# Layer 1 attention with every value product in plain single precision, keys in the index queries' buffer, and the sample's digit counts summed by a block transpose

## The chip, the cores and the metric

The kernel runs on one core of a Trainium2 chip. The metric is the device time of one execution in microseconds (us), the median of three runs. Instructions are issued on five engines: TensorE (PE; its weight loads are shown apart as PEld), VectorE (DVE), ScalarE (ACT), GpSimd (POOL) and SyncE (SP, which only issues DMAs).

## The reference, cut to what matters

One step of a two-layer decoder on a prompt of 1024 tokens and 8 sample tokens with 1024 cached tokens each. Layer 1 is the one that changes: 16 query heads over 4 key/value heads of width 64, where each query sees only the 256 keys that an indexer scores highest.

```python
score = jnp.einsum('bqhk,bqh->bqk', jax.nn.relu(dots), wi.astype(jnp.float32))
causal = kpos[None, None, :] <= qpos[None, :, None]
_, idx = lax.top_k(jnp.where(causal, score, -jnp.inf), topk)
...
s = jnp.einsum('bqngd,bqknd->bqngk', qg, k_sel).astype(jnp.float32) * (HEAD_DIM ** -0.5)
...
o = jnp.einsum('bqngk,bqknd->bqngd', p, v_sel)
```

The prompt has 8 blocks of 128 queries; a block i sees i+1 blocks of keys. Everything is in single precision.

## The kernel before

All work of layer 1 runs in streams: Python generators that yield an estimated time after each piece. A driver always continues the stream with the least virtual time, and a scheduler that simulates the program then fixes the order of instructions on each engine and the buffer of each tile. A tile waits for a free buffer of its kind. Each engine then runs its list strictly in that order.

The streams that meet around the change:

- The input projection (gen_main, dense_cols) multiplies in three products of split operands (L339 to L341, tiles d, xh, xl, whif, wlof). The weights of the next column tile are split ahead by ACT (whif) and DVE (wlof). The last tiles are queries, then keys (post_k), then values (post_v). The rotation of queries and keys runs on POOL (tiles raw, shf).
- The indexer (gen_idx, idx_scores) scores query blocks 2 to 7. top_select then finds each row's 256th score by 31 bisection steps, in pairs of blocks (2 and 3, 4 and 5, 6 and 7); each step is a count (L1983 on DVE, or an ACT pass with sign, tile tjk) and some operations on 128x2 elements (L226, L229, tile small). The result is a mask per block, written over the scores (tile sc).
- The sample stream (gen_dsa_dec) does the same for the 8 sample tokens, in 8 digit steps of 4 bits: 16 partitions of each sample try the 16 values of a digit, a count over 1025 scores (L2253) tells which hold, and a product with a constant matrix on PE (L2258, tile grpc) sums the outcomes of the 16 partitions. After the digits come ranks (transposed on PE at L2292, the rows "b<-small,hk"), one-hot lists and their product (L2314), then gathers of the chosen rows and their attention. The work area is the tile hk.
- The attention of the prompt (gen_attn, dsa_units, Unit) runs 32 units, query block i by key/value head g, in order of i. steps_a makes the scores (L530) and adds the mask (L533). steps_b transposes the exponentials in groups of one key block and four heads (L251, tile t), copies them out of PSUM (tile ph), and pv multiplies them with the values. The steps of a unit are interleaved with those of the unit before it.

Two forms of pv stand in the kernel. For blocks 0 to 4 (PLAIN) it is one single-precision product per group, 64 value columns by 512 (L2089, two records in the trace), and fin divides by the row sums, which are broadcast by a DMA through DRAM (d_ls, rv). For blocks 5 to 7 it is folded: ph holds a rounded high part and the low rest (made by ACT and by DVE, or by ACT and POOL through the tile pf where SPARE says so), the values stand in VS as high and low parts side by side, two reduced-precision products per group give 128 rows (L2093), and merge_out adds the halves, with the row sums brought over by two PE transposes (tiles rx, r). Blocks 5 to 7 have 4 x (6+7+8) = 84 groups in 12 units, blocks 0 to 4 have 60 groups in 20 units.

Four-part buffers (H, six of them): four hold the normalized activations, one the index queries and index keys (HX[0], tile hx, free once the last score is made, flag hx_free), one the sample's work area (HX[1], tile hk, free after L2314, flag hk_free). KS (split keys) and VS (split values) each need one later. The code for the keys is written after hk_free, that for the values after hx_free and the keys.

The out-projection (out1, on PE as L339 to L341 again) begins when all units and the samples are done (flags l1.att and l1.dec).

Of the kernel before, what the change touches and what calls it, by code (L numbers as in the profile page):

```python
# [32 lines left out]
def _consts():  # L33
# [32 lines left out]
    c["grp16"] = ((p[:, None] // 16 == p[None, :] // 16) & (p[:, None] % 16 >= 1)).astype(f)  # L66
# [9 lines left out]
def _r(ap):  # L76
    return ap.bitcast(F32)
# [17 lines left out]
SPARE = {3: (1,), 4: (1,), 5: (1, 3), 6: (1, 3), 7: (1, 3)}  # L95
BFC = True
PLAIN = range(5)
PMUL = ()
RXP = True
# [60 lines left out]
def build(tc, I, O, C):  # L160
    nc = tc.nc
    with ExitStack() as ctx:
# [1624 lines left out]
        def post_k(t, raw):  # L1787
            yield from rope(raw)
            nc.gpsimd.tensor_copy(out=K1[:, t], in_=raw[:, S:T])
            yield from need("hk_free")  # L1790
            if t == 0:
                KS[0] = H(F32R, "ks1")
            for e in range(2):
                split_stack(KS[0][:, 2 * t + e], raw, e, 0, S, gt)
            yield 2500.0
            flags.add("l1.k%d" % t)
            yield from nat_out(raw, O["dsa_kv_p"][0, 0, :, 0], t, O["dsa_kv_s"][0, :, 0, 0])

        def post_v(t, raw):
            yield 500.0  # L1800
            yield from need("l1.k1", "hx_free")
            if t == 0:
                VS[0] = H(F32R, "vs1")
            g = nat_out(raw, O["dsa_kv_p"][0, 0, :, 1], t, O["dsa_kv_s"][0, :, 0, 1],
                        [VS[0][:, 2 * t + e, :S].rearrange("p (i f) -> p i f", i=8) for e in range(2)], flip=False,
                        vn=VN1[:, t * 128:(t + 1) * 128], keep=VF)
            yield next(g)
            yield next(g)
            yield next(g)
            flags.add("l1.v%d" % t)  # L1810
            yield from g
# [228 lines left out]
        def dsa_units():  # L2040
# [8 lines left out]
            def make(i, g):  # L2049
# [21 lines left out]

                fold = i not in PLAIN
                d["u"] = 4 * i + g

                def pv(gr, ph):
                    kb = gr["kb"]
                    if kb == 0:
                        pst["o", i, g] = bank("o")
                        nc.vector.reciprocal(out=d["ls"], in_=d["ls"])
                        if fold:  # L2080
                            rx = pst["rx", i, g] = V([128, 4, 64], F32, "rx")
                            (nc.gpsimd if RXP else nc.vector).tensor_copy(out=rx, in_=d["ls"].unsqueeze(2).to_broadcast([128, 4, 64]))
                        else:
                            rv = pst["rx", i, g] = V([128, 512], F32, "rv")
                            dma(out=d_ls[i, g], in_=d["ls"])
                            dma(out=rv[:64], in_=d_ls[i, g].rearrange("q h -> (q h)").partition_broadcast(64))
                    po = pst["o", i, g]
                    if not fold:
                        mm(po[:64], lhsT=VF[g // 2][:, kb, 64 * (g % 2):64 * (g % 2) + 64], rhs=ph, start=(kb == 0), stop=(kb == i))  # L2089
                        return 860.0  # L2090
                    vs = VS[0][:, g, kb * 128:(kb + 1) * 128]
                    for x in range(2):
                        mm(po, lhsT=vs, rhs=ph[:, x], start=(kb + x == 0), stop=(kb == i and x == 1))  # L2093
                    return 430.0

                def fin():
# [4 lines left out]
                    if fold:  # L2101
                        yield from merge_out(ov[:, 0], ov[:, 1], lambda a: rx[:, 2 * a:2 * a + 2].rearrange("p e d -> p (e d)"),
                                             dh, dl, None)
                    else:
                        rw = rx[:64].rearrange("p (q a e) -> p e a q", a=2, e=2)
                        tm = V([128, 2, 128], F32, "tm")
                        pool = d["u"] % 8 in PMUL
                        if pool:
                            oc = V([128, 512], F32, "oc")
                            act(oc[:64], o[:64])  # L2110
                            ov = oc.rearrange("p (a e q) -> p e a q", a=2, e=2)
                            yield 500.0
                        for e in range(2):
                            (gt if pool else tt)(tm[64 * e:64 * e + 64], ov[:64, e], rw[:, e], MUL)
                        yield 700.0
                        act(dh, tm)
                        gt(dl, tm, _r(dh), SUB)
# [3 lines left out]
                u = Unit([tile_(hh) for hh in range(4)], groups, pv, start, fin, SPARE.get(i, ()) if fold else None)  # L2121
# [17 lines left out]
        def gen_dsa_dec():  # L2139
# [93 lines left out]
            grp = V([128, 128], F32, "grpc")  # L2233
            dma(out=grp, in_=C["grp16"])
# [11 lines left out]
            for step in range(8):  # L2246
# [8 lines left out]
                ts(cn, cn, TOPK - 0.5, None, ALU.is_ge)  # L2255
                yield DY
                p = bank()
                late(mm(p[:, 0:1], lhsT=grp, rhs=cn, start=True, stop=True))  # L2258
                yield 700.0
                sh_ = 28 - 4 * step  # L2260
                if step == 0:
                    ts(sf, p[:, 0:1], 7.5, -16.0, ALU.is_ge, MUL)
                    tt(sf, sf, p[:, 0:1], ADD)
                    ts(sh, sf, float(1 << sh_), None, MUL)
                else:
                    ts(sh, p[:, 0:1], float(1 << sh_), None, MUL)
# [20 lines left out]
            yield 26000  # L2287
# [23 lines left out]
            yield 4000  # L2311
# [310 lines left out]
```

## Time and profile before

| what | value |
|---|---|
| median of 3 runs | 2840.72 us (2839.03 to 2842.0) |
| the profiled execution, by the clock of the runs | 2849.54 us |
| its span, first to last instruction | 2847.5 us |
| busy share of PE, DVE, ACT, POOL | 90%, 79%, 47%, 47% |
| mean granted TensorE clock | 0.953 of full speed |

The profiled execution is 8.8 us above the median. A row of a view names line, engine and operation, then output <- inputs by tile names and the shape. "Idle before" is the time an engine stood still just before an instruction, put down to what ended it. All times in rows are in us from the start of the span, single durations in ns where a row says mean or min/median/max.

### The profile page before, as it was taken

The page shows a single profiled execution, that of the slowest core. Times are in us where ns is not written, and L with a number is a line of the kernel's source. Part 1 is how long each engine was busy: PE and PEld are TensorE (multiplying, and loading weights), DVE is VectorE, ACT ScalarE, POOL GpSimd, SP SyncE. Part 2 cuts the span into 40 slices and gives each one's busy share as a digit, 9 for nine tenths or more (in the row PEclk, how much of TensorE's full clock was granted, in tenths as well). Part 3 has the DMA queues.
Part 4 walks back from the last instruction along what each step waited for, and adds up shares of the span by engine and source line. Part 5 has one row for each costly group of instructions (what it writes and reads, how often), then busy time and mean ns, then how long its engine had stood idle before and what let it go on. Part 6 is the DMA issues. An engine that isn't in the chain of part 4 may idle for free.

```text
span 2847.5 us, 48497 instructions
## 1 busy us (share of the span) xinstructions
PE 2560.3 (90%) x17916; PEld 2391.2 (84%) x17916; DVE 2245.4 (79%) x4125; ACT 1330.8 (47%) x2726; POOL 1339.5 (47%) x992
## 2 busy tenths in 40 slices
PE   7988888989999899999888757999978999899998
PEld 6977788989999898999887743557978999898998
DVE  4476887778777889996469997998468887899995
ACT  4235756444433533332356566779434344533331
POOL 2375454245565557630445434224144656567630
PEclk8989999999999999999989878999989999999999
DMA  4844567303444633333353324311312343643431
GB/s 131 267 148 141 163 212 236 129 30 115 151 138 145 205 122 130 130 111 101 83 167 103 121 74 114 90 58 38 112 38 101 139 148 138 213 134 125 136 105 60
DMA packets 272095, 363.30 MB, mean 128 GB/s; under 512 B 25184, under 2 KB 200456, under 8 KB 271604
## 3 DMA queue, kind: packets, MB, share of 16 engines
q1 hardware_dynamic: 217124, 290.48, 32.0%
q0 software_dynamic: 15120, 49.81, 5.3%
q10 hardware_dynamic: 39616, 19.93, 2.4%
q8 instruction: 141, 2.31, 0.3%
q14 instruction: 94, 0.77, 0.1%
HBM read 252.19 MB, written 108.00 MB: 126 GB/s over the span
## 4 chain that ended last, share of the span: by engine, by line
PE 49%; DVE 20%; issue 5%; ACT 3%; DMA 2%; POOL 2%; SPq 0%; DVEq 0%; POOLq 0%; another core or an unknown queue 0%; ACTq 0%
PE d L1491 11%; PE d L1492 10%; PE d L1493 10%; DVE fdu L218 4%; PE d L341 3%; PE d L339 3%; PE d L340 3%; PE s L530 2%; PE t L251 2%; PE o L2089 1%; DVE xT L218 1%; DVE tjk L1983 1%; DVE x1a L218 1%; PE o L2093 1%; DVE fd L218 1%
## 5 line engine op out<-in xcount | busy, mean ns | idle before, releaser
L221 POOL TENSOR_TENSOR fraw<-fraw,small 128x1024 f32<-128x1024 f32 x64 | 137.9, 2160 | 196.7 <-DMA fraw<-in_ffn_w 163.0
L218 DVE TENSOR_TENSOR xT<-xT,d 128x258 f32<-128x258 f32 (+1 forms) x472 | 185.9, 424 | 52.9 <-PE d L341 32.8
L1491 PE MATMUL d<-xoph,fs 128*128 128x258 f32 x768 | 219.3, 286 | 8.6 <-ACT z L215 7.5
L1492 PE MATMUL d<-xoph,fs 128*128 128x258 f32 x768 | 218.3, 284 | 2.3 <-DVE xoph L218 2.3
L1493 PE MATMUL d<-xoph,fs 128*128 128x258 f32 x768 | 218.0, 284 | 2.1 <-DVE fs L218 2.1
L339 PE MATMUL d<-xh,whif 128*128 128x344 f32 (+1 forms) x616 | 201.7, 328 | 1.7 <-ACT xh L215 0.9
L341 PE MATMUL d<-xh,wlof 128*128 128x344 f32 (+1 forms) x616 | 197.2, 325 | 4.6 <-DVE wlof L218 4.6
L340 PE MATMUL d<-xl,whif 128*128 128x344 f32 (+1 forms) x616 | 200.3, 325 | 0.0
L221 POOL TENSOR_TENSOR z<-z 128x516 f32<-128x516 f32 x112 | 170.5, 1522 | 32.2 <-DMA d_zp<-z 21.9
L339 PE MATMUL d<-xh,whi 128*128 128x344 f32 x504 | 171.6, 341 | 10.9 <-ACT whi L215 5.6
L215 ACT ACTIVATE s<-s,small 128x128 f32<-128x128 f32 (+7 forms) x192 | 149.4, 782 | 65.9 <-DVE small L533 61.4
L341 PE MATMUL d<-xh,wlo 128*128 128x344 f32 x504 | 166.6, 333 | 12.0 <-DVE wlo L218 11.9
L340 PE MATMUL d<-xl,whi 128*128 128x344 f32 x504 | 168.6, 335 | 0.0
L218 DVE TENSOR_TENSOR fdu<-fraw,fdu 128x256 fp32r<-128x256 f32 x168 | 161.3, 971 | 0.0
L1491 PE MATMUL d<-xop,fl 128*128 128x258 f32 x512 | 147.2, 288 | 14.6 <-ACT fl L215 14.6
L1491 PEld LDWEIGHTS d<-xoph,fs 128*128 128x128 f32 x768 | 145.9, 190 | 10.3 <-ACT z L215 9.0
L1491 PE MATMUL d<-zoph,fdu 128*128 128x258 f32 x448 | 129.4, 291 | 23.8 <-DVE xT L218 12.1
L251 PE MATMUL t<-small,s 128*128 128x128 f32 x864 | 139.6, 280 | 12.1 <-DVE small L533 7.3
L1493 PEld LDWEIGHTS d<-xoph,fs 128*128 128x128 f32 x768 | 146.4, 191 | 2.7 <-DVE fs L218 2.5
L1492 PEld LDWEIGHTS d<-xoph,fs 128*128 128x128 f32 x768 | 146.1, 190 | 3.0 <-DVE xoph L218 3.0
L1493 PE MATMUL d<-xop,fl 128*128 128x258 f32 x512 | 145.9, 286 | 2.9 <-DVE fl L218 2.9
L1492 PE MATMUL d<-xop,fl 128*128 128x258 f32 x512 | 146.6, 286 | 0.0
(484 smaller groups left out, 9913.1 us busy)
## 6 DMA issues: line engine op xcount, KB each, us to landing
fraw<-in_ffn_w SPq DMA_DIRECT2D x120, 512.0 KB
zr<-d_zp SPq DMA_DIRECT2D x98, 516.0 KB
d_zp<-z POOLq DMA_DIRECT2D x56, 516.0 KB
kp<-in_cache_fox_kv SPq DMA_DIRECT2D x64, 256.0 KB
vp<-in_cache_fox_kv SPq DMA_DIRECT2D x64, 256.0 KB
q1b<-d_q ACTq DMA_DIRECT2D x32, 512.0 KB
d_zp<-z SPq DMA_DIRECT2D x28, 516.0 KB
wraw<-in_ab_w_in SPq DMA_DIRECT2D x21, 512.0 KB
```

Source lines behind the costliest of these rows:

```text
L215: return nc.scalar.activation(out=out, in_=in_, func=func, **kw)
L218: return nc.vector.tensor_tensor(out=out, in0=a, in1=b, op=op)
L221: return nc.gpsimd.tensor_tensor(out=out, in0=a, in1=b, op=op)
L251: return nc.tensor.transpose(out, in_, ident[:n, :n])
L339: mm(ps, lhsT=wh, rhs=ah, start=(j == 0), stop=False)
L340: mm(ps, lhsT=wh, rhs=al, start=False, stop=False)
L341: i = mm(ps, lhsT=wl, rhs=ah, start=False, stop=(j == last))
L530: mm(p[:, :m], lhsT=lh[x], rhs=ks[:, k0:k0 + m], start=(x == 0), stop=(x == 1 and not dg))
L1491: mm(o, lhsT=wh[:, k], rhs=hi[:, cols], start=(start and k == 0), stop=False, skip_group_check=not start)
L1492: mm(o, lhsT=wh[:, k], rhs=lo[:, cols], start=False, stop=False, skip_group_check=not start)
L1493: i = mm(o, lhsT=wl[:, k], rhs=hi[:, cols], start=False, stop=(k == nk - 1), skip_group_check=not start)
L1983: nc.vector.tensor_scalar(out=jk[:, 1, :n], in0=sj, scalar1=th, scalar2=None, op0=op, op1=ADD, accum_out=cnt[:, j:j + 1])
```

## The change

All blocks take the plain form of pv: the folded form, VS, SPARE and merge_out's use in layer 1 go. The keys' code is written after hx_free in place of hk_free. In the digit steps the PE product over 16 partitions goes; DVE spreads the outcome over 32 columns, transposes 32x32 blocks, multiplies by a constant and sums. Two estimates in the sample stream, after the ranks and after the one-hot lists, are longer by 6000 ns each, which places what follows later among the other streams.

```diff
--- before.py
+++ after.py
@@ -63,7 +63,8 @@
     c["bm8x64"] = np.ascontiguousarray(c["bm64"].T)
     c["bm64x128"] = (bh[:, None] // 8 == p[None, :] // 16).astype(f)
     c["bm8x128"] = (b8[:, None] == p[None, :] // 16).astype(f)
-    c["grp16"] = ((p[:, None] // 16 == p[None, :] // 16) & (p[:, None] % 16 >= 1)).astype(f)
+    f32 = np.arange(32)
+    c["grp32"] = ((p[:, None] % 32 // 16 == f32[None, :] // 16) & (f32[None, :] % 16 >= 1)).astype(f)
     c["bd16"] = (p[:, None] // 16 == p[None, :] // 16).astype(f)
     c["iot"] = np.concatenate([np.broadcast_to(np.arange(16, dtype=f), (128, 16)), p[:, None].astype(f)], 1)
     dig = np.zeros((128, 8), np.int64)
@@ -92,11 +93,7 @@
 ZSUB, ZLA = ("dpdpdpd", "p" * 7), 3
 UPE, DNE = ("dddd", "ddddddd"), ("pppp", "ddddddd")
 DNU = "vaavbbv"
-SPARE = {3: (1,), 4: (1,), 5: (1, 3), 6: (1, 3), 7: (1, 3)}
 BFC = True
-PLAIN = range(5)
-PMUL = ()
-RXP = True
 COP = "aad"
 NF = "p"
 KTE = "aa"
@@ -1787,7 +1784,7 @@
         def post_k(t, raw):
             yield from rope(raw)
             nc.gpsimd.tensor_copy(out=K1[:, t], in_=raw[:, S:T])
-            yield from need("hk_free")
+            yield from need("hx_free")
             if t == 0:
                 KS[0] = H(F32R, "ks1")
             for e in range(2):
@@ -1798,11 +1795,7 @@
 
         def post_v(t, raw):
             yield 500.0
-            yield from need("l1.k1", "hx_free")
-            if t == 0:
-                VS[0] = H(F32R, "vs1")
             g = nat_out(raw, O["dsa_kv_p"][0, 0, :, 1], t, O["dsa_kv_s"][0, :, 0, 1],
-                        [VS[0][:, 2 * t + e, :S].rearrange("p (i f) -> p i f", i=8) for e in range(2)], flip=False,
                         vn=VN1[:, t * 128:(t + 1) * 128], keep=VF)
             yield next(g)
             yield next(g)
@@ -2069,56 +2062,35 @@
                 groups = [dict(tr=[(hh * 128, lambda hh=hh, kb=kb: sm[hh][:, kb * 128:(kb + 1) * 128]) for hh in range(4)],
                                w=512, kb=kb) for kb in range(i + 1)]
 
-                fold = i not in PLAIN
-                d["u"] = 4 * i + g
 
                 def pv(gr, ph):
                     kb = gr["kb"]
                     if kb == 0:
                         pst["o", i, g] = bank("o")
                         nc.vector.reciprocal(out=d["ls"], in_=d["ls"])
-                        if fold:
-                            rx = pst["rx", i, g] = V([128, 4, 64], F32, "rx")
-                            (nc.gpsimd if RXP else nc.vector).tensor_copy(out=rx, in_=d["ls"].unsqueeze(2).to_broadcast([128, 4, 64]))
-                        else:
-                            rv = pst["rx", i, g] = V([128, 512], F32, "rv")
-                            dma(out=d_ls[i, g], in_=d["ls"])
-                            dma(out=rv[:64], in_=d_ls[i, g].rearrange("q h -> (q h)").partition_broadcast(64))
+                        rv = pst["rx", i, g] = V([128, 512], F32, "rv")
+                        dma(out=d_ls[i, g], in_=d["ls"])
+                        dma(out=rv[:64], in_=d_ls[i, g].rearrange("q h -> (q h)").partition_broadcast(64))
                     po = pst["o", i, g]
-                    if not fold:
-                        mm(po[:64], lhsT=VF[g // 2][:, kb, 64 * (g % 2):64 * (g % 2) + 64], rhs=ph, start=(kb == 0), stop=(kb == i))
-                        return 860.0
-                    vs = VS[0][:, g, kb * 128:(kb + 1) * 128]
-                    for x in range(2):
-                        mm(po, lhsT=vs, rhs=ph[:, x], start=(kb + x == 0), stop=(kb == i and x == 1))
-                    return 430.0
+                    mm(po[:64], lhsT=VF[g // 2][:, kb, 64 * (g % 2):64 * (g % 2) + 64], rhs=ph, start=(kb == 0), stop=(kb == i))
+                    return 860.0
 
                 def fin():
                     o, rx = pst.pop(("o", i, g)), pst.pop(("rx", i, g))
                     ov = o.rearrange("p (a e q) -> p e a q", a=2, e=2)
                     qs, hx, t0 = slice(i * 128, (i + 1) * 128), g // 2, 2 * g % 4
                     dh, dl = XH[hx][:, t0:t0 + 2, qs], XL[hx][:, t0:t0 + 2, qs]
-                    if fold:
-                        yield from merge_out(ov[:, 0], ov[:, 1], lambda a: rx[:, 2 * a:2 * a + 2].rearrange("p e d -> p (e d)"),
-                                             dh, dl, None)
-                    else:
-                        rw = rx[:64].rearrange("p (q a e) -> p e a q", a=2, e=2)
-                        tm = V([128, 2, 128], F32, "tm")
-                        pool = d["u"] % 8 in PMUL
-                        if pool:
-                            oc = V([128, 512], F32, "oc")
-                            act(oc[:64], o[:64])
-                            ov = oc.rearrange("p (a e q) -> p e a q", a=2, e=2)
-                            yield 500.0
-                        for e in range(2):
-                            (gt if pool else tt)(tm[64 * e:64 * e + 64], ov[:64, e], rw[:, e], MUL)
-                        yield 700.0
-                        act(dh, tm)
-                        gt(dl, tm, _r(dh), SUB)
+                    rw = rx[:64].rearrange("p (q a e) -> p e a q", a=2, e=2)
+                    tm = V([128, 2, 128], F32, "tm")
+                    for e in range(2):
+                        tt(tm[64 * e:64 * e + 64], ov[:64, e], rw[:, e], MUL)
+                    yield 700.0
+                    act(dh, tm)
+                    gt(dl, tm, _r(dh), SUB)
                     if i == 7 and g == 3:
                         flags.add("l1.att")
 
-                u = Unit([tile_(hh) for hh in range(4)], groups, pv, start, fin, SPARE.get(i, ()) if fold else None)
+                u = Unit([tile_(hh) for hh in range(4)], groups, pv, start, fin, None)
                 return u
 
             yield ("need", tuple("l1.%s" % x for x in ["k0", "k1", "v0", "v1"] + ["q%d" % t for t in range(8)] + ["in"]))
@@ -2230,8 +2202,9 @@
 
             dig = small("1", [128, 8], "digc", dt=I32)
             dma(out=dig, in_=C["dig"])
-            grp = V([128, 128], F32, "grpc")
-            dma(out=grp, in_=C["grp16"])
+            grp = V([128, 3, 32], F32, "grpc")
+            dma(out=grp[:, 0], in_=C["grp32"])
+            g32, c32, t32 = [grp[:, x] for x in range(3)]
             ti = [small("1", [128, 1], "tdi%d" % x, dt=I32) for x in range(4)]
             Pb, cd, sg, sh = ti
             cn, sf = small("1", [128, 1], "cnd"), small("1", [128, 1], "sfd")
@@ -2252,18 +2225,19 @@
                 tt(cd, cd, sh, ALU.bitwise_xor)
                 nc.vector.tensor_scalar(out=jk[:, :NK], in0=scd[:, :NK], scalar1=cd.bitcast(F32), scalar2=None,
                                         op0=ALU.is_ge, op1=ADD, accum_out=cn)
-                ts(cn, cn, TOPK - 0.5, None, ALU.is_ge)
+
+                ts(c32, cn.to_broadcast([128, 32]), TOPK - 0.5, None, ALU.is_ge)
+                nc.vector.transpose(t32, c32)
+                tt(t32, t32, g32, MUL)
+                nc.vector.tensor_reduce(out=cn, in_=t32, axis=AX.X, op=ADD)
                 yield DY
-                p = bank()
-                late(mm(p[:, 0:1], lhsT=grp, rhs=cn, start=True, stop=True))
-                yield 700.0
                 sh_ = 28 - 4 * step
                 if step == 0:
-                    ts(sf, p[:, 0:1], 7.5, -16.0, ALU.is_ge, MUL)
-                    tt(sf, sf, p[:, 0:1], ADD)
+                    ts(sf, cn, 7.5, -16.0, ALU.is_ge, MUL)
+                    tt(sf, sf, cn, ADD)
                     ts(sh, sf, float(1 << sh_), None, MUL)
                 else:
-                    ts(sh, p[:, 0:1], float(1 << sh_), None, MUL)
+                    ts(sh, cn, float(1 << sh_), None, MUL)
                 tt(Pb, Pb, sh, ALU.bitwise_or)
             tofloat(cd, Pb)
             th = cd.bitcast(F32)
@@ -2284,7 +2258,7 @@
             ts(new[:, 1:2], eq[:, S:NK], NEG, None, MUL)
             nc.vector.tensor_tensor_scan(out=rank[:, :S], data0=eq[:, :S], data1=eq[:, :S], initial=0.0, op0=ADD, op1=MAX)
             tt(rank[:, :S], rank[:, :S], eq[:, :S], MUL)
-            yield 26000
+            yield 32000
             tmp = V([128, 520], F32, "tmpd")
             rk = tmp[:, 0:64].rearrange("p (g b) -> p g b", g=8)
             for a in range(2):
@@ -2308,7 +2282,7 @@
                 yield 1200.0
             ol = oh[1].rearrange("p (g b) z -> p g b z", g=8)
             tt(ol, ol, pgf.rearrange("p (b g) -> p g b", b=8).unsqueeze(3).to_broadcast([128, 8, 8, 16]), MUL)
-            yield 4000
+            yield 10000
             p = bank()
             for g in range(8):
                 late(mm(p[:, :128], lhsT=rank[:, g * 128:(g + 1) * 128], rhs=eq[:, g * 128:(g + 1) * 128],
```

## Rows read from the trace of the kernel before

**Rows 1.** The page's head:
```profile
span 2847.5 us, 48497 instructions
```

**Rows 2.** Busy time by stretch: PE, PEld, DVE, ACT, POOL, clock, DMA share:
```profile
1500.00:1690.00 190.00, 135.39 (x740) 128.56 (x738) 176.00 (x373) 104.51 (x241) 91.03 (x49) 0.83 0.31 95
1690.00:1780.00 90.00, 64.09 (x239) 35.46 (x238) 72.17 (x272) 65.05 (x175) 31.59 (x35) 0.77 0.51 125
1780.00:1890.00 110.00, 108.03 (x500) 59.19 (x498) 101.48 (x292) 77.61 (x181) 20.11 (x20) 1.00 0.32 81
1890.00:2015.00 125.00, 118.70 (x683) 95.28 (x682) 107.16 (x272) 116.28 (x243) 53.59 (x58) 1.00 0.14 41
```

**Rows 3.** Instructions on tile ph: count, min/median/max ns, first and last start:
```profile
L2093 PE MATMUL o<-ph,vs x168: 388/397/507, 1890.1 to 2014.4; 128*128 128x512 f32 x168
...
L2089 PE MATMUL o<-ph,nat x120: 592/593/1116, 1706.6 to 1887.5; 128*64 128x512 f32 x120
```

**Rows 4.** PE in order of time, around a plain product (start, us):
```profile
1858.11 1.07 PE L2089 MATMUL o<-ph,nat 128*64 128x512 f32 x2
1859.11 0.73 PE L530 MATMUL s<-ks,q1b 128*128 128x512 f32 x2
```

**Rows 5.** PE in order of time, around folded products:
```profile
1956.41 1.09 PE L2093 MATMUL o<-ph,vs 128*128 128x512 f32 x4
1957.34 0.38 PE L251 MATMUL r<-small,rx 128*128 128x128 f32 x2
1957.56 0.60 PE L251 MATMUL t<-small,s 128*128 128x128 f32 x4
...
1959.87 0.71 PE L2093 MATMUL o<-ph,vs 128*128 128x512 f32 x2
1960.42 0.62 PE L530 MATMUL s<-ks,q1b 128*128 128x512 f32 x2
```

**Rows 6.** Groups on DVE, 1890 to 2015 (busy us, mean ns, idle before):
```profile
L218 DVE TENSOR_TENSOR ph<-t,ph 128x512 fp32r<-128x512 f32 x60 | 40.5, 687 | 2.7 <-ACT ph L215 2.1
```

**Rows 7.** Groups on DVE, 1780 to 1890:
```profile
L218 DVE TENSOR_TENSOR tm<-o,rv 64x256 f32<-64x256 f32 x24 | 14.5, 606 | 2.7 <-PE o L2089 2.3
L555 DVE COPY ph<-t 128x512 f32<-128x512 f32 x11 | 7.5, 682 | 0.0
...
L226 DVE TENSOR_SCALAR small<-small 128x2 int32<-128x2 int32 (+2 forms) x23 | 4.5, 194 | 0.4
```

**Rows 8.** The chain that ended last, the row sums' way through DRAM:
```profile
1704.01 1.93 DMA d_ls<-small
1705.95 4.31 DMA rv<-d_ls
```

**Rows 9.** Who PE waited for, 1500 to 1700 (total, times, longest):
```profile
PE b L2258 <- DVE small L226: 25.1, 5, 6.9
...
PE b L251 <- DVE hk L218: 8.5, 1, 8.5
```

**Rows 10.** PE in order of time, the product of the one-hot lists:
```profile
1668.18 3.76 PE L2314 MATMUL b<-hk 128*128 128x128 f32 x16 [13.69 <-DVE small L229]
```

**Rows 11.** Groups on DVE, 1500 to 1690:
```profile
L229 DVE SCALAR_TENSOR_TENSOR small<-small 128x2 int32<-128x2 f32 (+1 forms) x88 | 32.3, 377 | 9.6 <-ACT tjk L215 9.0
L226 DVE TENSOR_SCALAR small<-small 128x2 int32<-128x2 int32 (+4 forms) x97 | 31.9, 337 | 1.1
```

**Rows 12.** Who DVE waited for, 1500 to 1890, the longest:
```profile
DVE small L229 <- ACT tjk L215: 12.9, 11, 3.3
```

**Rows 13.** DVE in order of time, masks of blocks 6 and 7 written:
```profile
1889.93 0.39 DVE L226 TENSOR_SCALAR sc<-tjk 128x896 bf16<-128x896 bf16 x1
...
1903.98 0.63 DVE L226 TENSOR_SCALAR sc<-tjk 128x1024 bf16<-128x1024 bf16 x1
```

**Rows 14.** PE in order of time, first short score of block 6:
```profile
1919.00 0.51 PE L530 MATMUL s<-ks,q1b 128*128 128x384 f32 x2
```

**Rows 15.** Instructions on tile ks, those of layer 1 on ACT:
```profile
L215 ACT ACTIVATE ks<-raw x4: 1041/1050/1060, 1635.3 to 1671.6; 64x1024 fp32r<-64x1024 f32 x4
```

## The prediction

> **What bounds the kernel now.** I read the page's head first, for the span [rows 1], then the busy time by stretch from the first digit steps to the end of the prompt's attention [rows 2]. It shows two regimes. From 1500 to 1690 (input projection, index scores, digit steps, bisection) DVE is busy 176.0 of 190 us, while PE does 135.4 at a clock of 0.83. From 1690 to 1780 nothing is full, DVE is nearest to it with 72.2 of 90. From 1780 PE leads: 108.0 of 110 us (DVE 101.5), and from 1890, where the folded products start [rows 3], 118.7 of 125 at full clock, with DVE at 107.2 and ACT at 116.3. So time comes off the first part if DVE or its order allows it, and PE work added after 1890 is paid in full.
>
> The instructions on tile ph and PE in order of time give the price of either product [rows 3 to 5]. The list of who PE waited for gives what the sample stream costs it [rows 9, 10], and DVE's groups and waits say whether DVE could have been quicker [rows 11, 12].
>
> **The products of blocks 5 to 7.** A plain product occupies PE from 1858.11 to 1859.11, 1.00 us until the next instruction starts [rows 4]. A folded pair alone takes 1960.42 - 1959.87 = 0.55 us, and two pairs in a row take 1957.34 - 1956.41 = 0.93, or 0.465 each [rows 5]. Each of the 84 groups thus gains 0.45 to 0.535 us on PE: 37.8 to 45 us in all. I take 0.45, since mostly other work stands between pairs: +37.8. The transposes of the row sums go: 24 of them, at (1957.56 - 1957.34)/2 = 0.11 us each, -2.6. PE stands idle 125 - 118.7 = 6.3 us in this stretch [rows 2], and some of that goes with the longer chains of the fold; I credit 2.2 and bound it by 0 and 6.3. The last stretch grows by 37.8 - 2.6 - 2.2 = **33 us** (bounds 29 and 42).
>
> The other engines give no reason to soften this. DVE loses the 60 low parts (40.5 us, [rows 6]) and the half sums, and gains one copy in three of the groups, 24 at 0.682, and 24 divisions at 0.606 [rows 7]: 16.4 + 14.5 = 31 us. It ends at 107.2 - 40.5 + 31 = 98 or less. ACT hands those 24 copies to DVE and loses the passes through pf, so it ends at some 100 of 116.3. PE, at 118.7 + 33 = 152 us, leads by 50. The row sums of the 12 units now go through DRAM, 1.93 + 4.31 = 6.2 us [rows 8]; that is hidden under the unit's own products (125/12 = 10.4 us of PE per unit and more after the change), since only the final division needs them. Without that cover it would be 12 x 6.2 = 75 us at worst. The 24 DMAs queue on SP, behind which only the out-projection's weights wait.
>
> **The digit steps.** PE loses 8 products, and with them the waits for the count: 25.1 us in five waits [rows 9]. DVE gets three more operations a step (transpose, multiplication, sum; the comparison stays and becomes wider). Their shape is not in the trace. The nearest rows are the small operations, at a mean of 0.194 us late [rows 7] and 0.337 in this stretch [rows 11]: 24 of them cost 4.7 to 8.1 us. I take 6, as the tensors are 32 columns wide instead of two. The inflated mean goes with POOL, which is busy 91.0 us here against 20.1 from 1780 to 1890 [rows 2]. The Trainium skill (SBUF — State Buffer, section "SBUF: two separate sides") has it that VectorE and GpSimd share a port pair which whoever starts first holds for its whole instruction; the rows agree in sign. By the skill's rule the upper end, 8.1, would hold as long as POOL rotates queries beside, and the sum would be 2 us longer.
>
> **Ranks and one-hot lists later, keys earlier.** PE stood 8.5 us before the rank transposes [rows 9] and 13.69 before the one-hot product [rows 10], with projection work still to do behind. Both now stand 6 and 12 us later in the estimates, less 8 x 0.7 = 5.6 for the dropped waits in the digit steps, so 0.4 and 6.4 later in net: the second moves about half a column tile back in PE's list. The keys' split was only written after hk_free. The data did not wait for it: the first ran at 1635.3 [rows 15], ahead of the one-hot product at 1668.2 [rows 10], so it already had the index queries' buffer. What the edit frees is the order: the keys' raw tile and its transposes no longer stand behind the one-hot product, and single buffers come free earlier. I put no time of its own on it beyond the waits above. The dropped split of the values (ACT, POOL) is off the path. If a later one-hot list delays the sample's gathers, the prompt's units, which run to 2014 [rows 3], cover it.
>
> **What the front part gives back.** The waits on PE that can go are 25.1 + 8.5 + 13.7 = 47.3 us. But PE was waiting for DVE, and DVE was working. DVE's free time is 14.0 + 17.8 + 8.5 = 40.3 us over the first three stretches [rows 2]. Of it, 12.9 are waits for ACT's counts [rows 12], which the change doesn't touch, and 6 are filled with the new operations. That leaves 21. I take 16, three quarters, since PE will meet new waits further on. Bounds: 0 (PE only waits elsewhere for the same DVE work, such as the split weights) and 47.3.
>
> **Sum.** +33 - 16 = +17 us. Against the profiled execution's 2849.5 this is 2866.5; the median of the runs stands 8.8 lower, so the time to measure is 2840.7 + 17 = **2858 us**. One run's spread here is about 3 us; 0.2%, 5.7 us, is about what a measurement can tell from no change.
>
> **The rivals.**
>
> *PE breaks loose of DVE: faster.* Much of DVE's work before 1690 is bisection for blocks 6 and 7, whose masks are written at 1890 and 1904 [rows 13], while block 6's first short score comes at 1919 [rows 14]. There is slack of some 30 us, and with longer products in block 5 it grows by 24 x 0.45 = 11. If the scheduler, rid of eight points where PE and DVE must meet, orders the split weights ahead of bisection, all 47.3 us come back: 33 - 47 = -14, **2827 us**. It becomes faster once more than 33 + 5.7 = 39 us come back. For it: PE's own work needs only 135 of the first 190 us. Against: DVE is 93% busy there, and its total until mask 7 doesn't shrink.
>
> *Both sides meet: same.* The waits come back up to DVE's whole free time, 40.3 - 6 = 34 us. Net -1, **2840 us**. Against: the counts on ACT would have to stop holding DVE.
>
> *Nothing comes back.* DVE, with 6 us more to do, sets the projection's pace, and PE waits for split weights in place of digit counts. Net 33 to 39, **2876 us**. For it: DVE is busy 176.0 of the 190 us already, and its order need not change. Against: the 22 us before ranks and one-hot product are a matter of order, and the order moves.
>
> *PE is not full after 1890.* Weight loads cover only 95.3 of the 125 us [rows 2]; if the rest, 29.7, were room in which longer products hide, the last stretch would grow by 33 - 29.7 = 3 and the total be 2841 + 3 - 16 = **2828 us**. Against: PE shows 6.3 us of idle time, and the starts of [rows 4, 5] are one behind the other without a gap. The Trainium skill (Perfetto Trace Analysis, "Identifying the Most-Contended Engine") says matmul busy time is a poor measure of PE and weight loading a better one; by its rule this rival would hold. The trace speaks against it by the starts.
>
> **How the numbers follow.** The forecast, net +6 to +30, gets 0.48. Nothing comes back: 0.14. Same: 0.16. PE loose of DVE: 0.18; PE not full: 0.04. So slower 0.62, same 0.16, faster 0.22. The likeliest case's own range is 2847 to 2871. The range of 8 in 10 reaches down to 2828, which leaves out about half of the faster cases (0.11), and up to 2877, which leaves out about half of "nothing comes back" with large growth of the last stretch (0.08).
>
> **What would show it.** In the changed profile: from the first to the last product of block 5 to 7's values 150 to 162 us instead of 124.3 [rows 3], PE at 95% or more there, ACT and DVE well below. The first plain products of block 5 start 10 to 25 us earlier than 1890. No wait of PE on digit counts, but others on DVE in their place. DVE over 93% busy from 1500 to the end of the projection. The forecast is wrong if the projection ends more than 39 us sooner with the attention following it, if DVE's new operations cost over 0.5 us each, or if blocks 5 to 7 take less than 145 us.

## The result and the profile after

The changed kernel takes 2860.54 us (median of 4 runs, 2857.08 to 2864.88) against 2839.88 for the kernel before on the same chip: a ratio of 1.0076 [1.0061, 1.009], or about 21 us slower. The forecast was 2858. Its net of +17 came out of two terms that were both too small, and of opposite sign; that it lies so close is in part luck.

The page's head and busy time by stretch, cut where the projection, block 4 and block 5 end (columns as in [rows 2], two stretches left out):

```profile
span 2863.1 us, 48220 instructions
```

```profile
1500.00:1674.00 174.00, 132.74 (x740) 124.76 (x739) 164.89 (x343) 94.96 (x222) 93.05 (x48) 0.89 0.33 100
...
1869.00:1919.00 50.00, 48.64 (x203) 24.39 (x203) 46.13 (x124) 26.97 (x54) 3.03 (x4) 1.00 0.20 54
1919.00:2035.00 116.00, 115.81 (x456) 54.26 (x455) 58.56 (x150) 60.29 (x111) 5.85 (x8) 1.00 0.16 47
```

In the last two lines, blocks 5 to 7, PE is busy 164.45 of 166 us: full, at full clock. DVE has 104.7 of 166, ACT 87.3. The folded form needed 118.70 of 125 [rows 2]. The product's group and its neighbour in order of time:

```profile
L2075 PE MATMUL o<-ph,nat x288: 592/592/1116, 1688.2 to 2034.1; 128*64 128x512 f32 x144
```

```profile
1868.91 1.07 PE L2075 MATMUL o<-ph,nat 128*64 128x512 f32 x2
1869.91 0.51 PE L527 MATMUL s<-ks,q1b 128*128 128x256 f32 x2
```

The plain product costs 1.00 us here too [rows 4]. The first one of block 5 starts at 1868.91, where the first folded one started at 1890.1 [rows 3]; the last starts at 2034.1.

Who PE waited for from 1500 to 1750 (total, times, longest):

```profile
PE d L338 <- DVE wlof L215: 17.4, 5, 6.0
PE b L248 <- DVE hk L215: 6.6, 1, 6.6
```

The 25.1 us on digit counts [rows 9] are gone, and of the 13.69 on the one-hot lists [rows 10] 1.0 is left. The wait before the rank transposes is still there, 6.6 us where it was 8.5 [rows 9]. 17.4 us on DVE's split weights stand in place of the others, which were 1.2 before (from 1500 to 1700):

```profile
PE d L341 <- DVE wlof L218: 1.2, 1, 1.2
```

The new digit operations on DVE (groups of the first stretch: busy us, mean ns):

```profile
L215 DVE TENSOR_TENSOR grpc<-grpc 128x32 f32<-128x32 f32 x8 | 3.7, 464 | 0.0
...
L2230 DVE STREAM_TRANSPOSE grpc<-grpc 128x32 f32<-128x32 f32 x8 | 1.6, 204 | 0.0
L2232 DVE TENSOR_REDUCE small<-grpc 128x1 f32<-128x32 f32 x8 | 1.4, 180 | 0.1
```

3.7 + 1.6 + 1.4 = 6.7 us. The mask of block 7 is written 13.9 us later than in [rows 13]:

```profile
1917.90 0.42 DVE L223 TENSOR_SCALAR sc<-tjk 128x1024 bf16<-128x1024 bf16 x1
```

**The balance.** Three starts or ends in each trace cut it: the first product of layer 1's projection, the first value product of block 5, the end of the last value product. The front (first to second) went from 557.1 to 533.6 us, -23.5; the last stretch (second to third) from 124.7 to 165.8, +41.1. What lies ahead of layer 1 came 2.3 later and what follows the attention took 4.3 less, in work that the diff doesn't touch. -23.5 + 41.1 + 2.3 - 4.3 = +15.6, the difference of the two spans. The medians of the timed runs lie 20.7 apart: a trace is one execution, and the balance is one of traces.

In the front, PE's idle time fell from 103.0 to 83.9 us and its busy time from 454.1 to 449.7, at a mean granted clock of 0.90 in place of 0.88. DVE did less there, 434.7 us in place of 451.4, in spite of its new operations. Part of it is bisection that now comes later: from block 5's first product on, DVE spends 15.1 us on 37 of its operations, where it was 2.6 us on 3.

### The profile page after: what moved, and what is told of

The parts are those of the page before. It is cut to its first block, busy times and chain, and to the rows that moved or that the text cites. A ratio compares the mean times of both kernels' runs of the same rounds, so it can differ in the third digit from the quotient of the medians.

```text
span 2863.1 us, 48220 instructions
## 1 busy us (share of the span) xinstructions
PE 2602.7 (91%) x17876; PEld 2374.2 (83%) x17876; DVE 2226.5 (78%) x4113; ACT 1296.0 (45%) x2638; POOL 1284.4 (45%) x940
## 4 chain that ended last, share of the span: by engine, by line
PE 50%; DVE 19%; issue 5%; ACT 3%; DMA 2%; POOL 1%; SPq 0%; DVEq 0%; ACTq 0%; POOLq 0%
PE d L1488 10%; PE d L1489 10%; PE d L1490 10%; PE o L2075 4%; DVE fdu L215 4%; PE d L336 3%; PE d L338 3%; PE d L337 3%; PE s L527 2%; PE t L248 2%; DVE xT L215 1%; DVE tjk L1976 1%; DVE x1a L215 1%; DVE small L226 1%; DVE fd L215 1%
## 5 line engine op out<-in xcount | busy, mean ns | idle before, releaser
L1488 PE MATMUL d<-xop,fl 128*128 128x258 f32 x512 | 147.9, 289 | 14.6 <-ACT fl L212 14.6
L248 PEld LDWEIGHTS t<-small,s 128*128 128x128 f32 x864 | 102.9, 144 | 70.1 <-issue 41.1
L2075 PE MATMUL o<-ph,nat 128*64 128x512 f32 x288 | 153.3, 628 | 2.0 <-ACT ph L212 1.9
L1488 PEld LDWEIGHTS d<-xoph,fs 128*128 128x128 f32 x768 | 145.5, 189 | 9.1 <-ACT z L212 8.5
L218 POOL TENSOR_TENSOR xl<-tm,xh 128x256 fp32r<-128x256 f32 x32 | 23.5, 734 | 287.0 <-ACT xh L212 264.5
L1490 PE MATMUL d<-xop,fl 128*128 128x258 f32 x512 | 146.5, 288 | 2.5 <-DVE fl L215 2.5
L1490 PEld LDWEIGHTS d<-xoph,fs 128*128 128x128 f32 x768 | 146.0, 190 | 3.1 <-DVE fs L215 2.8
```

The costliest lines, as they stand in the source:

```text
L218: return nc.gpsimd.tensor_tensor(out=out, in0=a, in1=b, op=op)
L248: return nc.tensor.transpose(out, in_, ident[:n, :n])
L1488: mm(o, lhsT=wh[:, k], rhs=hi[:, cols], start=(start and k == 0), stop=False, skip_group_check=not start)
L1490: i = mm(o, lhsT=wl[:, k], rhs=hi[:, cols], start=False, stop=(k == nk - 1), skip_group_check=not start)
```

## The experiments

All twelve in these terms (us in the profiled execution; the ratio is from all timed runs):

| kernel | front | last stretch | both | ratio to the kernel before |
|---|---|---|---|---|
| before | 557.1 | 124.7 | 681.8 | 1 |
| changed | 533.6 | 165.8 | 699.4 | 1.0076 [1.0061, 1.009] |
| e1_digits | 541.3 | 132.9 | 674.2 | 0.9988 [0.9973, 1.0003] |
| e2_plain | 553.4 | 165.0 | 718.4 | 1.0118 [1.0099, 1.0136] |
| e3_front | 548.4 | 141.8 | 690.2 | 1.0022 [1.001, 1.0034] |
| e4_keys | 559.6 | 129.7 | 689.3 | 1.0024 [1.0009, 1.0038] |
| e5_skip | 538.0 | 137.9 | 675.9 | 0.9975 [0.996, 0.999] |
| e6_plain_digits | 547.9 | 163.5 | 711.4 | 1.0092 [1.0069, 1.0116] |
| e7_plain_keys | 552.2 | 163.9 | 716.1 | 1.0124 [1.009, 1.0157] |
| e8_pairs | 534.0 | 163.8 | 697.8 | 1.0063 [1.0036, 1.0089] |
| e9_spare | 544.1 | 139.8 | 683.9 | 1.0016 [0.9998, 1.0033] |
| e10_steps | 560.4 | 119.7 | 680.1 | 0.9967 [0.9948, 0.9986] |
| e11_short | 543.5 | 163.5 | 707.0 | 1.0083 [1.0052, 1.0115] |
| e12_fold_est | 546.3 | 141.8 | 688.1 | 1.0012 [0.9996, 1.0028] |

Each row but for the ratio is one execution. The stages ahead of layer 1 and behind the attention differ by up to 9.5 and 7.2 us between kernels that share them, so differences of a few us in a cell decide nothing, and where the ratio says less than the cells, the ratio counts.

**The value products alone.** Edit to the kernel before:

```diff
-PLAIN = range(5)
+PLAIN = range(8)
```

> The kernel before with plain products in blocks 5 to 7 too, and nothing else; the split values are still made, and not read. If the price is PE time after 1890, the time rises by 33 to 42 us, the first product of block 5 starts within 5 us of 1890, and the last stretch takes 158 to 166 us. Rival, the fold's departure also speeds the front or PE had room: a rise of less than 20 us.

The last stretch is 165.0, +40.3 with no other part of the change: the whole last term is the product. The front hardly moves. The first product of block 5 starts at 1881.6, 8.5 before the 1890.1, more than the 5 that were expected; 4.8 of it lie ahead of layer 1. The timed runs are 1.18% longer, some 34 us.

```profile
1882.00:2047.00 165.00, 165.00 (x655) 77.96 (x654) 91.30 (x236) 85.02 (x159) 8.14 (x12) 1.00 0.17 49
```

PE is busy in every microsecond while the weight loads take 77.96 of 165.

**Fewer products.** The changed kernel without 32 of the 84 value products of blocks 5 to 7:

```diff
-                    mm(po[:64], lhsT=VF[g // 2][:, kb, ...
+                    if i < 5 or kb % 2 == 0 or kb == i:
+                        mm(po[:64], lhsT=VF[g // 2][:, kb, ...
```

> The changed kernel without 32 of the 84 value products of blocks 5 to 7 (odd key blocks left out, except the last; the output of these blocks lacks them). All copies out of PSUM, masks and divisions stay. If PE time per product sets the last stretch, it falls by 32 x 1.0 = 32 us, from 166 to about 134, and the total by as much, to about 10 us below before. Rival, DVE, ACT or the chain from score to product is as near a bound: less than 16 us less than the changed kernel.

27.9 us of the last stretch went, 0.87 per product, and the time fell by 1%. PE then is no longer full: its idle time rose from 1.5 to 7.2 us, more than what is missing to the 32 expected:

```profile
1864.00:2002.00 138.00, 130.78 (x592) 71.80 (x592) 104.30 (x273) 86.76 (x164) 8.97 (x12) 0.99 0.19 51
```

With the page above this refutes "PE is not full after 1890".

**Two products in a row.** On PE, from block 5 on, each instruction's time until the next one starts, idle time left out, splits the +41.1: products 45.0 to 81.6 us (+36.6), transposes of the exponentials 31.7 to 38.2 (+6.5), scores 39.1 to 43.9 (+4.8), the 24 transposes of row sums -2.2, idle time 6.3 to 1.5 (-4.8). So the same transposes and scores take 11.3 us longer beside plain products.

The longer times stand where a plain product is the neighbour. A transpose takes 109 ns until the next transpose starts, in both kernels, and 28 until a folded product starts, but 202 until a plain one does (medians). Four transposes and the product behind them, before and after:

```profile
1892.17 0.60 PE L251 MATMUL t<-small,s 128*128 128x128 f32 x4
1892.52 0.71 PE L2093 MATMUL o<-ph,vs 128*128 128x512 f32 x2
```

```profile
1883.82 0.60 PE L248 MATMUL t<-small,s 128*128 128x128 f32 x4
1884.35 1.07 PE L2075 MATMUL o<-ph,nat 128*64 128x512 f32 x2
```

From the first transpose to the product it is 0.35 us before and 0.53 after. A score takes on average 309 ns right behind a plain product where it took 229 behind a folded one, and 286 right ahead of one where it took 198; elsewhere it is as before. By these means 42 transposes, 32 scores and 26 scores give 6.9 + 2.6 + 2.3 = 11.8 us, about the 11.3.

To see whether fewer such neighbours give time back, Unit's loop in the changed kernel keeps two groups back and issues their products one after the other:

```diff
-                        if prev:
-                            yield self.pv(*prev)
-                        prev = (g, ph)
+                        if z and z % 2 == 0:
+                            for h in held:
+                                yield self.pv(*h)
+                            held = []
+                        held.append((g, ph))
```

> The changed kernel with the plain products issued two in a row (the second group of a pair waits for nothing in between). A lone product took 1.00 us, two in a row 1.86, and the scores and transposes next to a product were some 0.02 us longer each than beside folded ones. If the change of number format between neighbours costs PE that, 72 pairs save 0.14 to 0.24 us each, 10 to 17 us, of which 6 to 10 in the last stretch. Rival, the longer lag between copy and product costs it back: within 4 us of the changed kernel.

2.0 us less in the last stretch, and a ratio whose interval covers the changed kernel's. But the pairs did not come about on PE: each product is still issued in a step of its own, and other work comes between. From block 5 on the 84 products stand there in 70 unbroken runs, 61 of them a single product, against 69 and 59 in the changed kernel; two rows that follow each other:

```profile
1930.38 1.07 PE L2080 MATMUL o<-ph,nat 128*64 128x512 f32 x2
1931.38 1.09 PE L248 MATMUL t<-small,s 128*128 128x128 f32 x8
```

Transposes and scores take 81.4 us (82.1 in the changed kernel). So this run does not test the expectation, and whether fewer neighbours would give time back stays open.

**The digits alone, with the fold.** The digit steps' part of the diff on the kernel before:

> The kernel before with the digit steps alone changed: the count's outcome is summed by the 32x32 block transpose on DVE in place of the product on PE; the folded products, the order of the keys and both longer estimates stay as before. If the meeting of PE and DVE at eight digit counts is what held the projection, the time falls by 10 to 21 us and the first attention product starts 10 to 18 us earlier. Rival, the keys' order and the later one-hot lists gave it back: within 5 us of before, with longer waits of PE before the rank transposes and the one-hot product.

The front shrinks by 15.8 and block 5's first product starts 17.5 us earlier, but the last stretch grows by 8.2, with the same products in it, and the time is the same (0.9988, interval to 1.0003). Block 5's stretch, 1872 to 1920:

```profile
1872.00:1920.00 48.00, 39.58 (x203) 30.53 (x203) 47.66 (x119) 36.10 (x77) 21.07 (x18) 0.93 0.15 45
```

DVE is busy 47.66 of 48 us and PE 39.58. The bisection that the front left undone (12.5 us on DVE from block 5 on, 2.6 before; mask 7 ends at 1919.4, not 1904.6) meets the fold's own work on DVE. In the changed kernel the same leftover meets plain products: PE full, DVE 46.13 of 50.

**All of the front, with the fold.** Digits, estimates and the keys after hx_free, on the kernel before; the values' split then has to follow hk_free, and only block 5 waits for it:

```diff
-            yield from need("hk_free")
+            yield from need("hx_free")
...
-            yield from need("l1.k1", "hx_free")
...
+            yield from need("l1.k1", "hk_free")
...
+                if i == 5 and g == 0:
+                    yield ("need", ("l1.vs0", "l1.vs1"))
```

> Everything of the change but the plain products: digit counts by the block transpose, longer estimates, keys after the index queries' buffer; the values' split is written after the one-hot product and asked for only by block 5, and blocks 5 to 7 stay folded. If front and last stretch are two separate terms, the time falls by 15 to 23 us below before, about 2819. Rival, the fold needs DVE, ACT and POOL that the front has only moved work to: less than 8 us below before.

Slower than before. More is put off (mask 7 ends at 1933.6) and more is paid back:

```profile
1877.00:1934.00 57.00, 40.58 (x210) 30.07 (x210) 56.06 (x136) 39.23 (x84) 18.04 (x18) 0.88 0.13 38
```

```profile
PE o L2102 <- DVE small L534: 11.0, 2, 10.6
```

DVE is full for 57 us, a value product waits 10.6 us for the mask addition in DVE's list, and the granted clock falls to 0.88 there. From 1500 to the attention's end DVE works 457.8 us here, 457.7 with the digits alone and 456.8 before.

**The keys' order and the later values' split, with the fold; no digits, estimates short.**

> The kernel before with the keys written after the index queries' buffer is free, and the values' split after the one-hot product and only asked for by block 5; digit counts stay on PE, estimates as before. By the theory that digit counts held PE: within 5 us of before. Rival, the order of the keys (their transposes and buffers behind the one-hot product) held the projection: 10 to 20 us below before.

Nothing comes back in the front (+2.5), and the time is 0.24% longer.

**Plain products with one more part each.** Three kernels fill the table between the products alone and the whole change: with the digits (keys and estimates as before), with keys and estimates (digits on PE), and with digits and keys but the short estimates.

> The kernel before with plain products everywhere and the digit counts by block transpose; keys after the work area, short estimates and the (unread) split values stay. If the digit counts make the whole front gain, it stands where the changed kernel does, 15 to 24 us above before (plain alone stood 34 above). Rival, the keys' order and estimates carry part of it: 27 us or more above before.

> The changed kernel with the digit counts back on PE (plain products, keys after the index queries' buffer, longer estimates stay). If the digit counts make the whole front gain, it stands 30 to 38 us above before, as plain alone did, and PE waits some 20 us on the counts again. Rival, order and estimates carry part: 27 us above or less.

```diff
-            yield 32000
+            yield 26000
...
-            yield 10000
+            yield 4000
```

> The changed kernel with the two estimates for ranks and one-hot lists put back to 26000 and 4000; digits by transpose, plain products and the keys' earlier order stay. From the start of layer 1's projection to block 5's first product it took 534 us in the changed kernel, 548 with plain products and digits alone, 552 with plain products, keys and estimates. Theory: the digits' partner is the keys' earlier order. Then this kernel keeps 530 to 538 us and a ratio to the kernel before within 0.0015 of the changed kernel's 1.0076. Rival: the partner is the later place of ranks and one-hot product in PE's order, behind which projection products otherwise wait. Then it takes 543 to 550 us, PE waits again for ranks or one-hot lists for 10 us or more, and the ratio is 1.009 to 1.012.

The front against e2_plain's 553.4: digits 5.5 less, keys and estimates 1.2 less, digits and keys 9.9 less, all three 19.8 less. In these traces the parts give more together than one by one: with the counts still on PE, the other two give next to nothing, and with the counts gone the one-hot lists remain, for which PE waits 6.1 us in e11_short and 1.0 in the changed kernel (for the ranks 7.0 and 6.6). The timed runs show less of it. The ratios are 1.0118 for the products alone, 1.0124 with keys and estimates, 1.0092 with digits, 1.0083 with digits and keys, 1.0076 with all; only the first and the last have intervals apart, and that difference is 0.0042, some 12 us, not 20. e11_short fits its rival by front and waits, its theory by the ratio; what the estimates bring is not shown.

**The same estimates with the fold.** The digits and the long estimates on the kernel before:

> The kernel before with the digits by transpose and the two longer estimates, and nothing else: folded products, stacked values and the keys' order as before. With the digits alone this took 541 us from the start of layer 1's projection to block 5 and 133 from there to the last value product, at a ratio of 0.9988. Theory: with the fold, time that comes back in the front is work of VectorE put off, and the fold's own VectorE work in blocks 5 to 7 takes it back. Then the first stretch shrinks to 530 to 540 us but the last grows to 133 to 142, and the ratio is 0.997 to 1.001. Rival: ranks and one-hot lists were a wait of order alone. Then the last stretch stays at 125 to 133 us, the sum of both is 8 us or more below the kernel with the digits alone, and the ratio is below 0.996: a kernel faster than both.

What was 9.9 us less of front beside plain products is a loss here: front 5.0 longer, last stretch 8.9 longer than with the digits alone, and a ratio 0.0024 above it, with intervals that just overlap. The expected shrinking of the front did not come. Mask 7 ends at 1932.5, and block 5 is held up as in e3_front, by waits and by the clock. From 6.3 us before, PE's idle time in the last stretch rose to 11.0, 19.7 and 17.6 (e1_digits, e3_front, e12_fold_est), its busy time from 118.4 to 121.9, 122.1 and 124.3, at mean granted clocks of 0.97, 0.95 and 0.94 where it had been 1.00. In e3_front the clock stood at its lower level (0.50 of full speed, 1.2 GHz) from 1912 to 1925, around the wait of 10.6 us.

```profile
1876.00:1936.00 60.00, 44.90 (x226) 34.05 (x225) 58.56 (x142) 41.59 (x90) 20.83 (x20) 0.86 0.12 36
```

**Less bisection.** The kernel before without the last 8 of 31 bisection steps of blocks 6 and 7, which asks whether DVE's total sets the front:

```diff
-            for b in range(30, -1, -1):
+            for b in range(30, 7 if grp[0] == 6 else -1, -1):
```

> The kernel before without the last 8 of 31 bisection steps of blocks 6 and 7 (their thresholds are left coarser). Some 8 x 1.9 = 15 us of DVE work go that no product needs early. If DVE's total work sets the front, block 5 starts 8 to 15 us earlier and the time falls by 6 to 15 us. Rival, PE's waits and order set it: less than 4 us.

```profile
1868.41 0.42 DVE L226 TENSOR_SCALAR sc<-tjk 128x1024 bf16<-128x1024 bf16 x1
```

Mask 7 is written 36 us earlier, yet in the trace block 5 starts no sooner (front +3.3), and the last stretch is 5.0 shorter. The time is 0.33% less, 9 us, which is inside what was expected if DVE's total sets the front. The two don't agree, and the traced execution took 2848.69 us, 10.5 above this kernel's median. So the trace speaks against the front being held by what DVE has to do until mask 7, but doesn't settle it.

**The fold's load on another engine.** The digits, and five groups in place of two of each unit of block 5 made by ACT and POOL:

```diff
-SPARE = {3: (1,), 4: (1,), 5: (1, 3), 6: (1, 3), 7: (1, 3)}
+SPARE = {3: (1,), 4: (1,), 5: (0, 1, 2, 3, 4), 6: (1, 3), 7: (1, 3)}
```

> The kernel with the digit counts by block transpose alone, where in block 5 five of six low parts (two before) go by ACT and POOL instead of DVE. In that kernel block 5 had DVE busy 47.7 of 48 us with PE at 39.6, since the bisection of the last pair ran on beside it. If the deferred bisection is what takes the front gain back, 12 groups x 0.69 = 8 us of DVE go and block 5 gets 5 to 8 us shorter: 8 to 12 us below before, faster than both kernels. Rival, ACT or POOL becomes the bound of block 5: within 3 us of the digit counts alone.

```profile
1878.00:1926.00 48.00, 35.59 (x184) 26.31 (x183) 41.51 (x98) 39.53 (x84) 36.40 (x28) 0.96 0.13 39
```

DVE is relieved, 41.51 of 48 us, but PE does less, 35.59, and the time is longer than with the digits alone (1.0016 against 0.9988, intervals that just overlap). No run here shows why PE does less. No version here is shown to be faster than the kernel before and computes the same: the digits alone come nearest, and their interval holds 1.

## Why the prediction was right, and where not

- **The last stretch, +33 (29 to 42): right in mechanism, sized too low.** Measured +41.1. The products gave +36.6 of the 37.8 counted: a record took 269 ns folded and 488 plain, or 0.54 and 0.98 a pair. The row sums' transposes gave back 2.2 of 2.6, and the stalls even 4.8 where 2.2 were credited. What the sum didn't have is the 11.3 us by which the neighbours on PE grew: it priced a product from its own start to the next one, 1.00 us, and left out what it costs the instruction ahead of it and the score behind it. The trace of before had that already: from 1780 to 1890 a transpose took 202 ns until a plain product started. "150 to 162 us" from first to last start was 165.2.
- **Other engines below PE: right.** DVE 104.7 and ACT 87.3 of 166; the 98 forecast for DVE left out the bisection that arrived later.
- **Digit steps, +6 on DVE (4.7 to 8.1): right**, 6.7. The reason given for the upper end holds for one of the three operations: 2.42 of the 6.7 us are one multiplication held beside POOL (last section).
- **The front, -16 (0 to 47): right in sign, too small.** Measured -23.5. "PE will meet new waits further on" is shown by the 17.4 us on split weights. What was off is the cap of 21 from DVE's free time: DVE wasn't held to its work until block 5, since bisection could be put off behind it (12.5 us more of it stand behind block 5's start than before), and the first stretch is only fuller (164.89 of 174, 94.8%). Of the 47.3 us of waits that it listed, the 8.5 before the ranks stayed at 6.6. How much each part gives is shown in traces only; the timed runs put digits, keys and estimates together at some 12 us beside plain products.
- **The keys' order at no time: not confirmed as a part by itself.** It gave nothing with the fold (e4_keys, where the later values' split comes with it) and some 4 us of front beside digits and plain products (e6_plain_digits against e11_short), about what such a difference can show.
- **The two terms added: right here, on a condition that the prediction didn't give.** It put a front and a last stretch side by side. In the traces of e1_digits, e3_front and e12_fold_est time gained in the front is partly bisection moved into block 5, and whether it is paid back there depends on the value product: with the fold, which needs DVE, the last stretch is 8 to 17 us longer; with the plain product, which fills PE and leaves DVE room, it is 165.8 against 165.0 without the moved bisection.
- **The sum: +17, measured +20.7 in timed runs and +15.6 between the traces.** The last stretch was 8 us too small and the front 7.5; that they cancel is luck.
- **The rivals.** "PE breaks loose" would have needed 39 us, "Both sides meet" 34. "Nothing comes back" named the right new wait, the split weights, but e6_plain_digits and the changed kernel show that it takes up only part of what the old ones held. "PE is not full" fell with e2_plain and e5_skip. The Trainium skill (Perfetto Trace Analysis, "Identifying the Most-Contended Engine") would judge PE's headroom by the share of weight loads, beside the share of peak arithmetic. The weight loads' share is 47% in e2_plain, in a stretch where PE had no idle time, and in the changed kernel less product work made that stretch shorter. So that share alone misleads here.

## What to carry to other kernels

Before a longer instruction on the full engine buys time elsewhere, price both in the stage where each is paid: here 23.5 us came back and 41.1 were spent. When several waits of one engine stand one behind the other, removing one can show little until the next is moved as well, so such parts are tried together and apart. The price of an instruction is read with its neighbours: here 11 us of it stood at the instructions ahead and behind. An experiment that changes the order is first read in the order that came out: e8_pairs changed the code and not PE's list. And time that an earlier stage gains by putting off work on a busy engine counts only if the stage that receives the work has room on that engine.

## What the runs showed of the hardware

Of the 24 operations of transposing, multiplying and summing, 23 took 0.17 to 0.21 us, and one multiplication 2.42, next to a GpSimd instruction (DVE, then POOL, in order of time):

```profile
1522.34 2.42 DVE L215 TENSOR_TENSOR grpc<-grpc 128x32 f32<-128x32 f32 x1
```

```profile
1521.47 3.22 POOL L218 TENSOR_TENSOR raw<-raw,ropc 128x1032 f32<-128x1032 f32 x1 [12.07 <-DVE shf L1754]
```

It started within POOL's instruction and ended at 1524.76, when that had ended at 1524.69. The first multiplication of the digit steps took 2.41 to 2.43 us in all nine kernels here that have the new steps. One of the eight comparisons took 1.33 us and ended 0.04 us after the POOL instruction within which it had started. Transposes and sums weren't held: those that started within a POOL instruction and ended long before it (at 1571.25, 1587.96 and 1592.89) took 0.17 to 0.20 us. The Trainium skill (SBUF — State Buffer, "SBUF: two separate sides") has it that VectorE and GpSimd share ports which one of them holds for its whole instruction, for a VectorE operation with two SBUF inputs or in one of its two-port modes; the multiplication, with two such inputs, agrees, and the held one is why its mean stands at 464 ns and its median at 186.

Beside plain products the neighbours on PE take longer, idle time left out: a transpose on average 119 ns in place of 99 until the next start, a score 264 in place of 235, at a granted clock of 1.00 in both stretches. It is the direct neighbours: 202 ns from a transpose to a plain product, 28 to a folded one. No run here shows why.
